# A hybrid decoder layer on one core: the order of work between the output projection and the up projection

## The chip, the cores and the metric

The kernel runs on one core of one Trainium2 chip. The metric is the device time of one execution in microseconds (us). Three runs of the kernel before took 1426.49, 1427.42 and 1429.19 us; the median is 1427.42.

Engines are named as the profile names them: PE is TensorE (PEld its weight loads), DVE is VectorE, ACT is ScalarE, POOL is GpSimd, SP is SyncE, which only issues transfers here. Each engine works through its own instructions in a fixed order and waits on semaphores of the others.

## The reference, cut to what matters

One layer: three groups of heads mix the sequence (not touched here), then

```python
h = h + jnp.concatenate([o_a, o_b, o_c], axis=-1) @ w_out[l]
h = h + conv_glu_ffn(rmsnorm(h, norm_ffn_g[l]), ffn_up[l], ffn_conv_w[l], ffn_conv_b[l], ffn_down[l])
gate = jax.nn.sigmoid(rmsnorm(h, norm_ple_g[l]) @ ple_gate[l])
h = h + gate * (p[l] @ ple_proj[l])

def rmsnorm(x, g):
    xf = x.astype(jnp.float32)
    y = xf * lax.rsqrt(jnp.mean(xf * xf, axis=-1, keepdims=True) + NORM_EPS)
    return (y * g.astype(jnp.float32)).astype(x.dtype)

def conv_glu_ffn(hn, w_up, conv_w, conv_b, w_down):
    u = hn @ w_up
...
    return (jax.nn.silu(gate) * val) @ w_down
```

The sequence has 1024 positions, the model 1024 columns, `D_FF` is 2816. The part left out of `conv_glu_ffn` is a causal depthwise convolution of width 3 over `u` (uc), whose halves are gate and val. All is float32.

## The kernel before, in words

Data lie transposed: a tile holds 128 columns of the model and all 1024 positions, so h is eight tiles h0 to h7, and a half is 512 positions (one bank of PSUM in float32).

**Products in split precision.** Every operand of a product is split into a high part (a copy of reduced width, `hi`, made by ACT as CAST) and a low part (source minus high part, `lo`, made by DVE or POOL as TENSOR_TENSOR). A product is three matmuls: high by high (L137), high weight by low data (L139), low weight by high data (L141) in `mm3`; in the up projection the three stand in `mul` (L1302). The weights' parts are `whi` and `wlo` (L114, L116), six buffers each in rotation.

**Output projection** (`phase_out`). `rows(m, halves)` makes row m of `@ w_out` for the named halves: 24 products a half into a bank pair `dp` (two in rotation), then DVE adds the bank to h (L1232) and ACT writes h out (L1233). Rows 0 and 1 are made for both halves at once, then rows 2 to 7 for the first half, then rows 2 to 7 for the second.

**Norm factors.** ACT squares the h tiles of a half, DVE sums them in `acc` (L216). `rstd` sums acc over partitions with four small matmuls (L183), DVE scales the sum (L186), POOL raises it to -1/2 (L190). `rstd_spread` spreads the factor over all partitions with four transposing matmuls (L196) into a bank `pb`. DVE then multiplies each h tile by the gain and pb (L1328, `ffn_norm`), and for the first half also splits it into the operands p1 (tiles 0 to 3) and p2 (tiles 4 to 7), called t0 to t15 in the profile (even numbers high, odd low). Before, the first half's factors are made in one piece between row 2 and row 3 of the second half, and the second half's in one piece behind row 7.

**Input embedding.** `p @ ple_proj` needs nothing of h, and is placed here: `pe_load` brings the two halves of p and of the weight (`praw`, two buffers) and splits them (`peh`, `pel`); `embed(m)` makes column m with 12 products, ACT copies the bank to `pst` (L1272, two buffers) and writes it out as `pe` m (L1273). Columns 0 to 4 go to the `dp` banks, 5 to 7 to the banks `bv` of the up projection.

**Operands of the up projection.** The up projection is one level of Strassen's scheme: 22 units f of column blocks, seven products each with the operands p1 to p7. `ffn_operands` makes, out of the normed tiles, the operands p6 and p5 (tiles tp6, tp5), and after the embedding's tiles are freed p7, p3 and p4 (tp7, tp3, tp4; `h` and `l` mark high and low part). The first two units' products with p1 and p2 are made here too; between them ACT keeps the p1 result as `e` (`keep_first`, L1390), since p2 adds into the same bank `bg`.

**Units** (`phase_up`). A unit has two bank pairs, G (`bg`) and V (`bv`). Its weights are sums of the four blocks of the weight: `s7`, `s6`, and for the third product `s6 + s2` (L1416), which may be made only when the sixth product's low part has been taken from s6. `x` (L1465) is e plus the second half of G, where the fifth product lies; the third product then adds into that half. L1467 adds x and the first half of V; the fourth product then adds into that half of V.

**What sets the order.** A scheduler puts the instructions of each engine in order by the place in the program and by dependence. `tc.issue_after(i)` holds an instruction behind the instruction i, `tc.high_priority(offset)` moves it forward by that many places.

## Time and profile before

| | |
|---|---|
| median of three runs | 1427.42 us |
| profiled execution | 1426.41 us, span 1424.6 us |
| mean granted clock of TensorE | 0.992 |
| PE busy | 1381.9 us (97%) |
| DVE busy | 1066.8 us (75%) |
| ACT busy | 602.5 us (42%) |
| POOL busy | 392.5 us (28%) |
| second half of the output projection to the first units | about 600 to 720 us of the span |

A row of the timeline has the start in us from the span's start, the duration, engine, line, operation, what it writes and reads, the count of like instructions that follow each other, and in brackets how long the engine stood idle before and what ended that. A wait is put down to the semaphore that came last by the records. A row of the waits has the waiting engine and line, what it waited for, then us in total, times, and the longest. Two matmuls overlap in the records, so their pace is read from start to start. The span begins with the first instruction and leaves out 1.8 us of the execution's time.

### The profile page before, as it was taken

To read this page: it belongs to the slowest core of one execution; us is meant where nothing else is said; L and a number is where in the kernel's file an instruction comes from. 1 tells how busy PE (TensorE), PEld (TensorE's weight loads), DVE (VectorE), ACT (ScalarE), POOL (GpSimd) and SP (SyncE) were. 2 spreads that over 40 slices of the span, in tenths; PEclk is the share of its full clock that TensorE was granted. 3 is DMA by queue.
4 is the path that set the end of the run, shared out by engine and by line. 5 is a ranking of instruction groups with operands and counts; after the bars stand their busy time and mean duration, and the time that the engine had idled before them with its cause. 6 is when DMAs were issued, how large, how long until landed. Compare 5 with 4: busy or idle time off the path is not lost.

```text
span 1424.6 us, 22342 instructions
## 1 busy us (share of the span) xinstructions
PE 1381.9 (97%) x8642; PEld 1118.0 (78%) x8642; DVE 1066.8 (75%) x1629; ACT 602.5 (42%) x1015; POOL 392.5 (28%) x286
## 2 busy tenths in 40 slices
PE   8989999999999999999999999999999999999996
PEld 6768777777778768787788888888888888888885
DVE  7597363964666796468788888898888799778675
ACT  7411323123155485254544444443434444455542
POOL 5321012210122141221244544454543000002431
PEclk9999999999999999999999999999999999999998
DMA  6124111240432211753332233333324963441443
GB/s 220 45 82 119 61 46 61 81 119 32 154 143 104 84 61 40 262 178 117 119 111 91 94 106 102 106 102 111 112 96 147 356 214 111 126 141 47 135 158 113
DMA packets 80122, 167.61 MB, mean 118 GB/s; under 512 B 19984, under 2 KB 22288, under 8 KB 80016
## 3 DMA queue, kind: packets, MB, share of 16 engines
q1 hardware_dynamic: 66496, 146.52, 30.6%
q10 hardware_dynamic: 12656, 16.52, 3.4%
q0 software_dynamic: 864, 3.15, 0.6%
q8 instruction: 68, 1.11, 0.3%
q14 instruction: 38, 0.31, 0.1%
HBM read 119.76 MB, written 46.40 MB: 117 GB/s over the span
## 4 chain that ended last, share of the span: by engine, by line
PE 48%; issue 3%; DVE 2%; POOL 1%; ACT 1%; DMA 0%; POOLq 0%; ACTq 0%; DVEq 0%
PE bg L1302 16%; PE bv L1302 12%; PE bv L1596 7%; PE bg L1596 7%; PE dp L141 1%; PE dp L137 1%; PE dp L139 1%; POOL wlo L116 1%; PE bv L137 0%; PE bv L139 0%; PE bv L141 0%; DVE h L1692 0%; POOL xh L162 0%; DVE gt L1691 0%; ACT whi L114 0%
## 5 line engine op out<-in xcount | busy, mean ns | idle before, releaser
L137 PE MATMUL dp<-xh,whi 128*128 128x512 f32 x544 | 189.2, 408 | 6.9 <-DVE r L501 2.9
L139 PE MATMUL dp<-xl,whi 128*128 128x512 f32 x544 | 182.7, 396 | 0.8 <-DVE xl L411 0.8
L141 PE MATMUL dp<-xh,wlo 128*128 128x512 f32 x544 | 181.1, 394 | 0.0
L116 POOL TENSOR_TENSOR wlo<-wraw,whi 128x512 fp32r<-128x512 f32 x60 | 81.6, 1360 | 321.4 <-ACT whi L114 257.1
L116 POOL TENSOR_TENSOR wlo<-raw,whi 128x512 fp32r<-128x512 f32 x84 | 134.7, 1622 | 76.0 <-ACT whi L114 76.0
L114 ACT CAST whi<-wraw 128x512 fp32r<-128x512 f32 x120 | 72.8, 617 | 155.7 <-PE dp L139 107.3
L1302 PE MATMUL bg<-t,whi 128*128 128x512 f32 x352 | 133.3, 389 | 0.0
L137 PEld LDWEIGHTS dp<-xh,whi 128*128 128x128 f32 x544 | 99.4, 189 | 34.9 <-issue 6.2
L139 PEld LDWEIGHTS dp<-xl,whi 128*128 128x128 f32 x544 | 102.2, 189 | 23.8 <-DVE xl L411 1.1
L141 PEld LDWEIGHTS dp<-xh,wlo 128*128 128x128 f32 x544 | 102.7, 189 | 22.9 <-issue 0.8
L116 POOL TENSOR_TENSOR wlo<-s,whi 128x512 fp32r<-128x512 f32 x44 | 64.0, 1454 | 175.0 <-ACT whi L114 175.0
L1596 PE MATMUL bg<-t,whi 128*128 128x512 f32 x308 | 95.3, 390 | 0.0
L1596 PE MATMUL bv<-t,whi 128*128 128x512 f32 x308 | 94.8, 389 | 0.0
L114 ACT CAST whi<-raw 128x512 fp32r<-128x512 f32 x88 | 52.6, 619 | 94.3 <-issue 48.3
L114 ACT CAST whi<-s 128x512 fp32r<-128x512 f32 x66 | 38.9, 620 | 121.4 <-PE bg L1302 113.6
L1302 PEld LDWEIGHTS bg<-t,whi 128*128 128x128 f32 x352 | 66.1, 188 | 13.6
L190 POOL TENSOR_TENSOR rst<-rst,mhalf 128x4 f32<-128x4 f32 (+1 forms) x9 | 9.9, 1102 | 235.6 <-DVE rst L186 218.5
L1302 PE MATMUL bg<-t,wlo 128*128 128x512 f32 x176 | 67.2, 389 | 0.0
L1596 PEld LDWEIGHTS bv<-t,whi 128*128 128x128 f32 x308 | 57.9, 188 | 11.9
L1596 PEld LDWEIGHTS bg<-t,whi 128*128 128x128 f32 x308 | 57.8, 188 | 12.0
L1592 ACT CAST t<-t 128x512 fp32r<-128x512 f32 x77 | 47.8, 622 | 45.5 <-PE bv L1596 31.8
L116 DVE TENSOR_TENSOR wlo<-wraw,whi 128x512 fp32r<-128x512 f32 x60 | 49.7, 829 | 20.6 <-ACT whi L114 20.4
(417 smaller groups left out, 3415.1 us busy)
## 6 DMA issues: line engine op xcount, KB each, us to landing
raw<-in_ffn_up_dram SPq DMA_DIRECT2D x44, 512.0 KB, 3.5
wraw<-in_w_in_dram SPq DMA_DIRECT2D x28, 512.0 KB, 3.4
z<-zst SPq DMA_DIRECT2D x18, 512.0 KB, 2.8
gb<-ct SPq DMA_DIRECT2D x33, 256.0 KB, 2.2
t<-gb SPq DMA_DIRECT2D x33, 256.0 KB, 2.7
t<-gt SPq DMA_DIRECT2D x33, 256.0 KB, 2.7
zl<-z SPq DMA_DIRECT2D x16, 512.0 KB, 4.2
wraw<-in_ple_gate_dram SPq DMA_DIRECT2D x16, 512.0 KB, 3.4
```

The costliest lines, as they stand in the source:

```text
L114: self.cast = nc.scalar.copy(hi, src).ins
L116: eng.tensor_tensor(lo, src, hi.bitcast(F32), ALU.subtract)
L137: nc.tensor.matmul(ps[hf], wh, xh[hf], start=first, stop=False)
L139: nc.tensor.matmul(ps[hf], wh, xl[hf], start=False, stop=False)
L141: nc.tensor.matmul(ps[hf], wl, xh[hf], start=False, stop=last)
L190: nc.gpsimd.tensor_tensor(r2, r, self.mhalf[:, :n], ALU.pow)
L1302: nc.tensor.matmul(ps, w[part == 2][:, s], X[k][part == 1], start=start and k == part == 0, stop=k == 3 and part == 2, skip_group_check=no ...
L1592: nc.scalar.copy(xh, x)
L1596: nc.tensor.matmul(ps[m], wt[part == 2][:, m * P:(m + 1) * P], (xh, xl)[part == 1], start=k == part == 0, stop=k == NK - 1 and part == 2)
```

## The change

Five edits, none of which adds or drops a product, a copy or a transfer:

1. The first half's factors are made up to POOL's power behind row 2, and spread behind row 3. The loop over rows starts at 4 and takes two `pe_load` in its first turn.
2. The second half's factors are made and spread inside the embedding's second column: the sum behind its first six products, the spread behind its last six.
3. ACT's copy of an embedding column is moved forward in the order by 400 places.
4. In `ffn_operands` the second part of the first units' weights is split ahead of the p1 products; p7 is split first, the copies `e` are held behind the last cast before them, p3 is split in two pairs between, and p4 behind the p2 products.
5. In unit 1 the sum `s6 + s2` is held behind x of unit 0.

```diff
@@ phase_out
         rows(2, (1,))
-        pb = self.rstd_bcast(acc, 1.0 / 1024, EPS, self.mxp)
+        ps, pb = (self.mxp.tile([P, n], F32, tag="mx", name=self.nm("ps_ss")) for n in (4, HT))
+        r = self.rstd(ps, (acc,))
+        rows(3, (1,))
+        pb = self.rstd_spread(r, pb)
...
-        for m in range(3, ND):
+        for m in range(4, ND):
             rows(m, (1,))
             for _ in range(2):
                 next(norm, None)
-            if parts:
-                self.pe_load(pwp, *parts.pop(0))
+            for _ in range(2 if m == 4 else 1):
+                if parts:
+                    self.pe_load(pwp, *parts.pop(0))
         for m in range(ND):
             self.sq_acc(acc, self.h[m][:, HT:], m == 0)
-        pb = self.rstd_bcast(acc, 1.0 / 1024, EPS, self.mxp)
+        ps, pb = (self.mxp.tile([P, n], F32, tag="mx", name=self.nm("ps_ss")) for n in (4, HT))
         self.ffn_first()
+        r = []
+        hooks = {(1, 0): lambda: r.append(self.rstd(ps, (acc,))), (1, 1): lambda: self.rstd_spread(r[0], pb)}
         for m in range(5):
-            self.embed(m, pw, px, self.dps.tile([P, T], F32, tag="dp", name=self.nm("dp")))
+            self.embed(m, pw, px, self.dps.tile([P, T], F32, tag="dp", name=self.nm("dp")), hooks)
@@ embed
+            if (m, k) in hooks:
+                with self.tc.issue_after(self.step):
+                    hooks[m, k]()
         t = self.wpool.tile([P, T], F32, tag="wraw", name=self.nm("pst"), bufs=2)
-        self.nc.scalar.copy(t, ps)
+        with self.tc.high_priority(offset=400):
+            self.nc.scalar.copy(t, ps)
@@ ffn_operands
-        self.mul(*[(d["G"][:, :HT], d["w1"], self.TX["p1"], True) for d in first])
-        for d in first:
-            self.keep_first(d)
         for d in first:
             d["w2"] = self.split2(d["raw"][:, HT:], V)
-        self.mul(*[(d["G"][:, :HT], d["w2"], self.TX["p2"], False) for d in first])
+        self.mul(*[(d["G"][:, :HT], d["w1"], self.TX["p1"], True) for d in first])
...
-        for n, B in (("p7", B12), ("p3", B22), ("p4", B21)):
-            for k in range(4):
-                split(n, k, B[k])
+        for k in range(4):
+            split("p7", k, B12[k])
+        for i, d in enumerate(first):
+            with self.tc.issue_after(self.cast):
+                self.keep_first(d)
+            for k in (0, 1):
+                split("p3", 2 * i + k, B22[2 * i + k])
+        self.mul(*[(d["G"][:, :HT], d["w2"], self.TX["p2"], False) for d in first])
+        for k in range(4):
+            split("p4", k, B21[k])
@@ w, in phase_up
             if n == "3":
-                V.tensor_tensor(d["s"]["3"], d["s"]["3"], d["s"]["2"], ALU.add)
+                with ExitStack() as order:
+                    if d["f"] == 1:
+                        order.enter_context(self.tc.issue_after(self.units[0]["x"]))
+                    V.tensor_tensor(d["s"]["3"], d["s"]["3"], d["s"]["2"], ALU.add)
```

(`self.step` is the last matmul of `mm3`, `self.cast` the last cast of `op_split`, `d["x"]` the instruction that makes x.)

**TensorE at the second half's factors.** Before (dp_1170 and dp_1172 are the embedding's first two columns; the peh numbers ending in 22 and 44 are the two halves of the embedding's weight, 30 and 44 after):

```order
L137 MATMUL dp_1172_6584<-peh_1122_6340,peh_1133_6391 128x512 x2
L183 MATMUL ps_ss_1158_6538<-few_78,acc_5825 128x1 x4
L139 MATMUL dp_1172_6584<-pel_1123_6341,peh_1133_6391 128x512 x2
L196 MATMUL ps_ss_1159_6539<-cst_76,rst2_1161_6546 128x128 x4
L141 MATMUL dp_1172_6584<-peh_1122_6340,pel_1134_6392 128x512 x2
```

Now:

```order
L137 MATMUL dp_1170_6572<-peh_1130_6377,peh_1133_6385 128x512 x2
L139 MATMUL dp_1170_6572<-pel_1131_6378,peh_1133_6385 128x512 x2
L141 MATMUL dp_1170_6572<-peh_1130_6377,pel_1134_6386 128x512 x2
L183 MATMUL ps_ss_1158_6538<-few_78,acc_5825 128x1 x4
L137 MATMUL dp_1170_6572<-peh_1144_6436,peh_1148_6477 128x512 x2
L139 MATMUL dp_1170_6572<-pel_1145_6437,peh_1148_6477 128x512 x2
L141 MATMUL dp_1170_6572<-peh_1144_6436,pel_1149_6478 128x512 x2
L196 MATMUL ps_ss_1159_6539<-cst_76,rst2_1172_6585 128x128 x4
```

The sum stands four products later in the second column, and six products instead of two stand between the sum and the spread.

**ACT at the end of the embedding.** Before (pst_1187, 1189 and 1191 are the copies of columns 5, 6 and 7):

```order
L1320 CAST tp6h3_6664<-nu_1183_6695 128x512
L1320 CAST tp5h6_6670<-h2_5795 128x512
L1320 CAST tp5h7_6672<-h3_5796 128x512
L1272 COPY pst_1187_6724<-bv_1186_6711 128x1024
L1272 COPY pst_1189_6740<-bv_1188_6727 128x1024
L1273 DMA pe5_6289<-pst_1187_6724 128x1024
L1273 DMA pe6_6290<-pst_1189_6740 128x1024
L1320 CAST tp7h0_6836<-h0_5793 128x512
L1272 COPY pst_1191_6756<-bv_1190_6743 128x1024
L1320 CAST tp7h1_6838<-h1_5794 128x512
```

and, after the write of column 7 and the cast of tp7h2:

```order
L1390 COPY e_1192_6783<-bg_1184_6709 128x512
L1390 COPY e_1193_6785<-bg_1185_6710 128x512
L1320 CAST tp7h3_6842<-h3_5796 128x512
L1320 CAST tp3h0_6828<-h4_5797 128x512
```

Now, from the copy of column 5 to the first casts of p3 in two pieces:

```order
L1282 COPY pst_1187_6724<-bv_1186_6711 128x1024
L1330 CAST tp5h5_6668<-h1_5794 128x512
L1330 CAST tp5h6_6670<-h2_5795 128x512
L1330 CAST tp6h3_6664<-nu_1183_6695 128x512
L1282 COPY pst_1189_6740<-bv_1188_6727 128x1024
L1330 CAST tp5h7_6672<-h3_5796 128x512
L1283 DMA pe5_6326<-pst_1187_6724 128x1024
L1283 DMA pe6_6327<-pst_1189_6740 128x1024
L1330 CAST tp7h0_6808<-h0_5793 128x512
L1282 COPY pst_1191_6756<-bv_1190_6743 128x1024
L1330 CAST tp7h1_6810<-h1_5794 128x512
```

```order
L1330 CAST tp7h2_6812<-h2_5795 128x512
L1330 CAST tp7h3_6814<-h3_5796 128x512
L1404 COPY e_1196_6832<-bg_1184_6709 128x512
L1330 CAST tp3h0_6800<-h4_5797 128x512
L1330 CAST tp3h1_6802<-h5_5798 128x512
L1404 COPY e_1197_6838<-bg_1185_6710 128x512
```

The copy of column 5 stands ahead of the casts of tp5h5, tp5h6 and tp6h3; all casts of tp7 stand ahead of the two copies e, which lie among the casts of p3. The copy of column 7 still stands ahead of the cast of tp7h1.

**VectorE between the units.** Before (s7_1213 and s6_1214 belong to unit 1, s7_1234 and s6_1235 to unit 2, x_1208 and bv_1206 to unit 0):

```order
L116 TENSOR_TENSOR wlo_1205_6976<-s7_1198_6961,whi_1204_6974 128x512
L1408 TENSOR_TENSOR s7_1213_7029<-raw_1164_6556,raw_1165_6558 128x512
L1455 TENSOR_TENSOR v_1207_6991<-e_1192_6783,bv_1206_6978 128x512
L1410 TENSOR_TENSOR s6_1214_7031<-s7_1213_7029,raw_1165_6558 128x512
L1411 TENSOR_TENSOR raw_1165_6558<-raw_1165_6558 128x512
L1416 TENSOR_TENSOR s6_1214_7031<-s6_1214_7031,raw_1164_6556 128x512
L1465 TENSOR_TENSOR x_1208_7005<-e_1192_6783,bg_1184_6709 128x512
L116 TENSOR_TENSOR wlo_1220_7044<-s7_1213_7029,whi_1219_7042 128x512
L1408 TENSOR_TENSOR s7_1234_7142<-raw_1226_7125,raw_1227_7127 128x512
L1410 TENSOR_TENSOR s6_1235_7144<-s7_1234_7142,raw_1227_7127 128x512
L1467 TENSOR_TENSOR bv_1206_6978<-x_1208_7005,bv_1206_6978 128x512
```

Now, from the sum of the weight's last block on:

```order
L1425 TENSOR_TENSOR raw_1163_6546<-raw_1163_6546 128x512
L1482 TENSOR_TENSOR x_1208_7005<-e_1196_6832,bg_1184_6709 128x512
L1433 TENSOR_TENSOR s6_1214_7031<-s6_1214_7031,raw_1162_6544 128x512
L116 TENSOR_TENSOR wlo_1220_7044<-s7_1213_7029,whi_1219_7042 128x512
L1422 TENSOR_TENSOR s7_1234_7142<-raw_1226_7125,raw_1227_7127 128x512
L1424 TENSOR_TENSOR s6_1235_7144<-s7_1234_7142,raw_1227_7127 128x512
L1484 TENSOR_TENSOR bv_1206_6978<-x_1208_7005,bv_1206_6978 128x512
```

x and the sum have changed places; L1467 (now L1484) stands behind the same instructions as before.

8 lines of the change are left out of this document (4 added, 4 removed).

## The prediction

> **What bounds the kernel now.** I read the view by stages first, then TensorE's waits between 615 and 760 us, then the timelines there, engine by engine. In the loop over the column blocks TensorE has no free time (columns: stretch, us, then busy us of PE, PEld, DVE, ACT, POOL, granted clock, DMA share, GB/s):
>
> ```profile
> 800.00:900.00 100.00, 100.00 (x443) 82.83 (x442) 88.13 (x90) 42.28 (x59) 48.66 (x31) 1.00 0.33 111
> ```
>
> So time that TensorE loses ahead of this loop moves everything behind it. All its named waits there lie where the change works:
>
> ```profile
> PE bg L1302 <- ACT whi L114: 1.9, 1, 1.9
> PE ps_ss L196 <- POOL rst L190: 1.3, 2, 0.8
> PE bv L137 <- ACT pst L1272: 0.8, 1, 0.8
> PE ps_ss L183 <- DVE acc L216: 0.6, 1, 0.6
> PE bv L1302 <- DVE bv L1467: 0.3, 1, 0.3
> ```
>
> These are 4.9 us, but the timeline shows more. I measure from start to start: products that run without a wait follow each other by 0.227 us (0.453 us for a pair).
>
> ```profile
> 629.18 0.39 PE L139 MATMUL dp<-xl,whi 128*128 128x512 f32 x1
> 630.12 0.65 PE L196 MATMUL ps_ss<-cst,rst 128*128 128x128 f32 x4 [0.55 <-POOL rst L190]
> ...
> 659.45 0.61 PE L137 MATMUL dp<-peh,peh 128*128 128x512 f32 x2
> 660.62 1.02 PE L183 MATMUL ps_ss<-few,acc 128*128 128x1 f32 x8 [0.56 <-DVE acc L216]
> 661.50 0.72 PE L139 MATMUL dp<-pel,peh 128*128 128x512 f32 x2
> 662.98 0.65 PE L196 MATMUL ps_ss<-cst,rst 128*128 128x128 f32 x4 [0.76 <-POOL rst L190]
> 663.38 0.99 PE L141 MATMUL dp<-peh,pel 128*128 128x512 f32 x2
> ...
> 667.34 0.62 PE L139 MATMUL dp<-pel,peh 128*128 128x512 f32 x2
> ...
> 680.49 0.39 PE L1302 MATMUL bg<-t,whi 128*128 128x512 f32 x1
> 681.66 0.73 PE L137 MATMUL bv<-peh,peh 128*128 128x512 f32 x2 [0.78 <-ACT pst L1272]
> ...
> 703.10 0.39 PE L1302 MATMUL bv<-tp7h,wlo 128*128 128x512 f32 x1
> 705.43 0.47 PE L1302 MATMUL bg<-tp3h,whi 128*128 128x512 f32 x1 [1.95 <-ACT whi L114]
> ...
> 708.24 0.39 PE L1302 MATMUL bv<-tp6h,whi 128*128 128x512 f32 x1
> 708.98 0.50 PE L1302 MATMUL bv<-tp4h,whi 128*128 128x512 f32 x1 [0.35 <-DVE bv L1467]
> ```
>
> Lost: 630.12 - 629.18 - 0.23 = 0.71; 660.62 - 659.90 = 0.72; 662.98 - 661.95 = 1.03; five pairs from 663.38 to 667.34 take 3.96 instead of 2.27, so 1.69; 0.94 at 681.66; 2.10 at 705.43; 0.51 at 708.98. That is 7.7 us. The 1.69 are no wait: the granted clock is down there.
>
> ```profile
> 664.00:668.00 4.00, 4.00 (x12) 3.13 (x12) 4.00 (x7) 1.02 (x1) 0.00 (x0) 0.62 0.02 9
> ```
>
> **The change, on TensorE.** No product, copy or transfer is added or taken away; all is moved. The first factors' spread (L196) goes behind row 3's 24 products (5.4 us), the factor is there by 630.12 and TensorE comes at 629.41 + 19 x 0.227 = 633.7: minus 0.71. The second acc sum (L183) goes four products back, which is 0.91 us, while the 0.71 brings TensorE forward: it comes at 659.90 - 0.71 + 0.91 = 660.10. It waits for the end of this VectorE queue:
>
> ```profile
> 656.92 0.69 DVE L1232 TENSOR_TENSOR h<-h,dp 128x512 f32<-128x512 f32 x1 [1.29 <-PE dp L141]
> 658.10 1.77 DVE L1416 TENSOR_TENSOR s<-s,raw 128x512 f32<-128x512 f32 x1 [0.48 <-POOL wlo L116]
> 659.79 0.68 DVE L216 TENSOR_TENSOR acc<-acc,sqt 128x512 f32<-128x512 f32 x1
> ```
>
> All three follow row 7's end (its addition is the first row), now 0.71 earlier, so acc lets L183 start at 659.91: no wait, 0.2 to spare. From L183's start to L196's were 2.36 us (660.62 to 662.98); L183's own 0.88 and six products (1.36) now stand between, 2.24, so 0.12 is left of the 1.03. The half-rate stretch follows from a TensorE that, between 659.9 and 663.4, had one pair of products beside L183 and two waits; with nine products there I expect full rate, minus 1.69. Of the embedding products the eighth waits for a bank that ACT copies out; that copy stood behind three casts and now stands ahead of three, so that it ends near 676.2 where TensorE comes at 676.5 (662.46, 0.40 for L196 and five embedding products of 12 x 0.227): minus 0.94.
>
> At 705.43 the page names the cast of a weight. I read it otherwise: tp3's products add into the half of the G bank that x reads, and x ends at 704.61 + 0.68 = 705.29. TensorE starts 0.14 later. x stood behind L1416 of unit 1, which waited for GpSimd; x now goes first. On TensorE alone the sum of all is 7.7 - 0.12 = 7.6.
>
> **The same change on VectorE, which I think decides.** tp4's first product waits for L1467, and L1467 stands at the end of a VectorE queue that is nearly full from the second factors on:
>
> ```profile
> 663.67 5.35 DVE L1328 SCALAR_TENSOR_TENSOR h<-h,par,ps_ss 128x512 f32<-128x512 f32 x8 [1.83 <-PE ps_ss L196]
> ...
> 674.10 0.69 DVE L1321 TENSOR_TENSOR tp6l<-nu,tp6h 128x512 fp32r<-128x512 f32 x1 [1.46 <-ACT tp6h L1320]
> ...
> 687.80 1.29 DVE L1321 TENSOR_TENSOR tp7l<-h,tp7h 128x512 fp32r<-128x512 f32 x2 [2.17 <-ACT tp7h L1320]
> 691.32 0.69 DVE L1321 TENSOR_TENSOR tp7l<-h,tp7h 128x512 fp32r<-128x512 f32 x1 [2.23 <-ACT tp7h L1320]
> ...
> 696.75 0.68 DVE L116 TENSOR_TENSOR wlo<-s,whi 128x512 fp32r<-128x512 f32 x1
> ...
> 702.95 1.74 DVE L1416 TENSOR_TENSOR s<-s,raw 128x512 f32<-128x512 f32 x1 [1.52 <-POOL wlo L116]
> 704.61 0.68 DVE L1465 TENSOR_TENSOR x<-e,bg 128x512 f32<-128x512 f32 x1
> ...
> 708.23 0.69 DVE L1467 TENSOR_TENSOR bv<-x,bv 128x512 f32<-128x512 f32 x1
> ```
>
> Call W the start of the weight's low part at 696.75. From 663.67 to W are 33.1 us, of which three waits take 5.9 (6.1 from issue to issue, since each also breaks an overlap of 0.09): 27.0 us of work. L196 comes at 660.10 + 2.36 = 662.46, 0.52 earlier; so without any wait W would be 663.15 + 27.0 = 690.1. Behind W the chain stays: L1416 starts 6.20 after W, because it needs the low part that GpSimd makes from a sum that VectorE makes after W,
>
> ```profile
> 701.62 1.29 POOL L116 TENSOR_TENSOR wlo<-s,whi 128x512 fp32r<-128x512 f32 x1 [1.34 <-ACT whi L114]
> ```
>
> and L1467 starts 5.28 after L1416, of which 0.60 was x. x now lies in the 1.52 that VectorE waits for GpSimd, so it costs nothing, and tp4 starts 6.20 + 4.68 + 0.75 = 11.63 after W.
>
> What waits does W keep? The three were ACT's doing:
>
> ```profile
> 680.61 1.91 ACT L1272 COPY pst<-bv 128x1024 f32<-128x1024 f32 x2
> 681.64 1.24 ACTq L1273 DMA_DIRECT2D pe<-pst  x2
> 686.23 1.01 ACT L1272 COPY pst<-bv 128x1024 f32<-128x1024 f32 x1 [1.35 <-DMA pe<-pst]
> 689.70 1.07 ACT L1390 COPY e<-bg 128x512 f32<-128x512 f32 x2 [1.41 <-PE bg L1302]
> 693.26 2.19 ACT L1320 CAST tp4h<-h 128x512 fp32r<-128x512 f32 x4
> DMA to landing us min/median/max: 2.6/3.0/4.8
> ```
>
> A copy takes ACT 0.93 us, a cast 0.52. The 1.46 goes: tp6h's first cast no longer stands behind a copy that waits for TensorE. The 2.17 stays in part: tp7h1 still stands behind the eighth embedding copy, and that behind the landing of the sixth's write, whose buffer it takes. In the new order 21 instructions stand between the factors and the last nu (8 at 5.35 / 8 = 0.66, 13 at 0.60: it starts at 676.3 and ends at 676.9); then ACT has a cast, a copy and a cast, and issues the write at about 679.0. From issue to the copy that waited took 4.6 us in the trace (681.64 to 686.23, two writes together); with the median landing it is 3.0. So the eighth copy starts at 682.0 to 683.6 and tp7's second low part 1.6 later, 683.6 to 685.2, where VectorE, 12 instructions behind 676.3, would be at 683.5: a wait of 0.1 to 1.7. The 2.23 goes, since tp7's casts now stand ahead of the e copies; but each e copy takes a place between tp3's casts, and VectorE, at 0.60 an instruction, runs into them for about 0.3 twice. New waits: 0.7 to 2.3.
>
> Sum: 0.52 + 6.1 + 0.60 - (0.7 to 2.3) = 4.9 to 6.5. The write goes out in a pair again, as in the row with 4.6, so I take a value near the lower end, **5.2**. TensorE's 7.6 is more than this, so tp4 waits for the rest: about 2.4 us of idle there, where tp3 waited before. VectorE and GpSimd also collide (L1416 took 1.77 and 1.74 beside a GpSimd low part, 0.68 is a like instruction alone): such collisions lie behind W before and after, and one more or less is 1.1 us either way. That bounds the sum at 3.8 and 7.6.
>
> At no cost: the embedding operands' low parts, drawn forward on VectorE to where it now waits for row 3, while the factor's eight multiplications go back by 3.6 us. The queue holds the same instructions up to row 7's addition, ahead of which 1.29 us were idle; the earlier end of row 7 takes 0.71 of that. If the cover were gone, L183 would be late by what is lacking.
>
> **Base.** The profiled execution took 1426.41 us (span 1424.60), the median of the runs is 1427.42. 1426.41 - 5.2 = 1421.2 for an execution like that; on the median, **1422.2 us**. A measurement of this kernel tells about 0.2%, 2.9 us, from no change.
>
> **Rivals.** (a) *VectorE meets no wait and no extra collision*: then TensorE's 7.6 or VectorE's 7.2 is the gain, 1420.0. For: casts are 0.52 and VectorE's 0.60. Against: the write's landing. 15%.
>
> (b) *The half rate moves to tp4.* In the trace 1.75 us of waits within 3.5 us (660 to 663.4) were followed by 3.9 us at half rate, while 2.10 at once (703.3 to 705.4) were not. A wait of 2 to 3 us at tp4 lies between; if the clock falls, 1.7 go back: gain 3.5, 1423.9. 18%. [...]
>
> (c) *ACT stays the bound*: the eighth copy's write lands late (4.8 or more) and the e copies come late, so VectorE keeps its 6.1 us of waits. Then only 0.52 + 0.60 come, 1426.3: no change. 12%.
>
> (d) *Slower.* The last half of the embedding weight is now cast ahead of t0's cast on ACT. Its load can be issued only when VectorE has done the first half's low parts (about 631.1), and behind that cast ACT holds the t casts, row 7's weights and the squares that feed acc. The load took 3.3 us:
>
> ```profile
> praw<-in_ple_proj_dram SPq DMA_DIRECT2D x1, 512.0 KB, 3.3
> ```
>
> That gives 634.4, as ACT comes. About 0.8 us (0.58 of idle left, 0.2 to spare) is covered, the rest delays L183 one for one. It decides from 641, ten us after the issue; at 645 the time would be 1431. Against it: three times the measured time would be needed. 5%.
>
> **Chances.** Forecast 50%. Faster by over 0.2% are the forecast, (a) and most of (b): 0.79; within it (c) and the rest: 0.16; slower 0.05. Range: from (a) with the spread of the runs, 1419.2, to between (b) and (c), 1425.7. The forecast's own is 1420 to 1423.7.
>
> **What would show it.** Right: no wait before L196 near 634 and under 0.3 before it near 662; clock 1.00 from 660 to 668; no wait at the eighth embedding product; tp3's first product behind tp7 without a wait, and a wait of 2 to 3 us before tp4 on L1467's line; W near 692. Wrong: a W near 690 with TensorE still late (the work count), tp3 still late with x done (my reading of 705.43), or half rate behind tp4 (b).

## The result and the profile after

Six runs of the changed kernel took 1419.75 to 1422.87 us, median 1421.09; six of the kernel before, beside them, 1425.96 to 1429.41, median 1426.95. The ratio is 0.9953, 95% interval 0.9941 to 0.9964: 5.9 us faster by the medians, 5.1 to 8.4 by the interval. The prediction was 1422.2 (1419.2 to 1425.7), a gain of 5.2. The profiled execution took 1421.0 us, span 1419.2.

TensorE's waits between 615 and 760 us, of which the kernel before had five (columns as there):

```profile
PE bv L1312 <- DVE bv L1484: 1.2, 1, 1.2
```

One is left, before tp4. L1484 is the addition into V (L1467 before), L1482 is x, L1433 the sum s6 + s2, L1338 the factor's multiplications, L1312 the products. TensorE's timeline of the change:

```profile
628.38 0.94 PE L183 MATMUL ps_ss<-few,acc 128*128 128x1 f32 x8
...
634.78 0.60 PE L196 MATMUL ps_ss<-cst,rst 128*128 128x128 f32 x4
...
661.09 0.95 PE L183 MATMUL ps_ss<-few,acc 128*128 128x1 f32 x8
...
663.39 0.64 PE L196 MATMUL ps_ss<-cst,rst 128*128 128x128 f32 x4
...
699.04 0.39 PE L1312 MATMUL bv<-tp7h,wlo 128*128 128x512 f32 x1
699.26 0.39 PE L1312 MATMUL bg<-tp3h,whi 128*128 128x512 f32 x1
...
701.98 0.39 PE L1312 MATMUL bv<-tp6h,whi 128*128 128x512 f32 x1
703.58 0.50 PE L1312 MATMUL bv<-tp4h,whi 128*128 128x512 f32 x1 [1.21 <-DVE bv L1484]
```

Neither factor makes TensorE wait, tp3 follows tp7 at the normal pace of 0.22 us, and tp4 loses 703.58 - 701.98 - 0.23 = 1.37 us. The granted clock (third column from the right, 1.00) does not fall behind the second factors:

```profile
660.00:664.00 4.00, 4.00 (x25) 3.35 (x24) 0.90 (x3) 1.36 (x2) 1.01 (x1) 1.00 0.66 233
664.00:668.00 4.00, 4.00 (x20) 3.27 (x19) 3.93 (x6) 1.61 (x2) 0.00 (x0) 1.00 0.40 162
```

VectorE's timeline, the rows that answer to those of the prediction:

```profile
664.07 5.35 DVE L1338 SCALAR_TENSOR_TENSOR h<-h,par,ps_ss 128x512 f32<-128x512 f32 x8 [1.83 <-PE ps_ss L196]
...
686.77 1.29 DVE L1331 TENSOR_TENSOR tp3l<-h,tp3h 128x512 fp32r<-128x512 f32 x2 [0.49 <-ACT tp3h L1330]
688.30 1.29 DVE L1331 TENSOR_TENSOR tp3l<-h,tp3h 128x512 fp32r<-128x512 f32 x2 [0.23 <-ACT tp3h L1330]
...
691.92 0.68 DVE L116 TENSOR_TENSOR wlo<-s,whi 128x512 fp32r<-128x512 f32 x1
...
696.74 0.69 DVE L1482 TENSOR_TENSOR x<-e,bg 128x512 f32<-128x512 f32 x1
698.13 1.76 DVE L1433 TENSOR_TENSOR s<-s,raw 128x512 f32<-128x512 f32 x1 [0.70 <-POOL wlo L116]
...
702.84 0.68 DVE L1484 TENSOR_TENSOR bv<-x,bv 128x512 f32<-128x512 f32 x1
```

Of the three waits on ScalarE (1.46, 2.17, 2.23) none is left; two small ones are new (0.49, 0.23). x lies ahead of the sum, in what was the wait for GpSimd.

**One measure for all kernels.** The start of the first factors' product (L183 near 628 us) differs between executions, so I measure from there to tp4's first product, and from there to the end of the span. In the two profiled executions:

| | first factors | tp4 | stretch | tp4 to the end | sum |
|---|---|---|---|---|---|
| before | 627.35 | 708.98 | 81.63 | 715.62 | 797.25 |
| change | 628.38 | 703.58 | 75.20 | 715.62 | 790.82 |

(The span is read to 0.1 us, so the last two columns are good to 0.05.) The stretch gained 6.43 us, and nothing is won or lost behind it. The span gained 5.4, because the changed kernel's execution came to the stretch 1.03 us late, in code that the change does not touch: its TensorE ran at half rate (granted clock 0.50) from 360.36 to 363.78 us. Of the fourteen executions in this document, the four without half rate between 16 and 600 us (before, e1, e3, e7) come to the stretch at 627.29 to 627.40, the ten with such stretches at 628.05 to 632.86.

### The profile page after: what moved, and what is told of

Its sections match the earlier page's. It is cut to its first block, busy times and chain, and to the rows that moved or that the text cites. A ratio compares the mean times of both kernels' runs of the same rounds, so it can differ in the third digit from the quotient of the medians.

```text
span 1419.2 us, 22340 instructions
## 1 busy us (share of the span) xinstructions
PE 1380.7 (97%) x8642; PEld 1117.5 (79%) x8642; DVE 1066.0 (75%) x1629; ACT 603.2 (43%) x1015; POOL 393.3 (28%) x286
## 4 chain that ended last, share of the span: by engine, by line
PE 64%; DVE 4%; issue 3%; POOL 2%; ACT 2%; DMA 1%; SPq 0%; POOLq 0%; ACTq 0%; DVEq 0%
PE bg L1312 17%; PE bv L1312 12%; PE bv L1613 7%; PE bg L1613 7%; PE dp L139 3%; PE dp L137 3%; PE dp L141 3%; PE swq L1143 1%; PE hsc L990 1%; PE zp L137 1%; PE zp L141 1%; PE zp L139 1%; PE swo L1183 1%; PE swt L1169 1%; PE bv L139 1%
## 5 line engine op out<-in xcount | busy, mean ns | idle before, releaser
L1312 PE MATMUL bg<-t,whi 128*128 128x512 f32 x352 | 133.4, 389 | 0.0
L1312 PEld LDWEIGHTS bg<-t,whi 128*128 128x128 f32 x352 | 66.1, 188 | 13.8
L1312 PE MATMUL bg<-t,wlo 128*128 128x512 f32 x176 | 67.5, 389 | 0.0
```

What stands on the lines that cost most here:

```text
L1312: nc.tensor.matmul(ps, w[part == 2][:, s], X[k][part == 1], start=start and k == part == 0, stop=k == 3 and part == 2, skip_group_check=no ...
```

## The experiments

All kernels in one table, times in us from the profiled executions; the ratio to the kernel before is given with its interval where runs were timed. The ratios are of three batches (e1 to e4; the change again and e5 to e7; e9), each with its own runs of the kernel before, so only those of one batch compare closely. The kernel before again, e3 again and e4 again are one execution each.

| kernel | first factors | tp4 | stretch | tp4 to the end | sum | ratio |
|---|---|---|---|---|---|---|
| before, again | 632.86 | 714.56 | 81.70 | 715.64 | 797.34 | |
| change, again | 628.05 | 703.24 | 75.19 | 715.66 | 790.85 | 0.9935 (0.9911 to 0.9959) |
| e1 sum ahead of x | 627.32 | 702.62 | 75.30 | 715.48 | 790.78 | 0.9956 (0.9940 to 0.9973) |
| e2 fifth edit alone | 630.32 | 710.16 | 79.84 | 715.44 | 795.28 | 0.9984 (0.9973 to 0.9995) |
| e3 edits 1, 2 alone | 627.40 | 704.95 | 77.55 | 717.15 | 794.70 | 0.9983 (0.9968 to 0.9999) |
| e3 again (e12) | 631.49 | 709.05 | 77.56 | 715.45 | 793.01 | |
| e4 edits 3, 4 alone | 628.64 | 707.74 | 79.10 | 715.66 | 794.76 | 1.0000 (0.9988 to 1.0012) |
| e4 again (e11) | 629.99 | 710.71 | 80.72 | 715.39 | 796.11 | |
| e5 edit 2 undone | 628.60 | 704.65 | 76.05 | 715.65 | 791.70 | 0.9960 (0.9943 to 0.9976) |
| e6 edit 1 undone | 631.08 | 707.02 | 75.94 | 715.68 | 791.62 | 0.9950 (0.9933 to 0.9967) |
| e7 addition into V earlier | 627.29 | 701.11 | 73.82 | 716.89 | 790.71 | 0.9937 (0.9917 to 0.9957) |
| e9 and x of unit 2 earlier | 628.59 | 702.41 | 73.82 | 715.59 | 789.41 | 0.9938 (0.9913 to 0.9962) |

Two executions of one program agree in the stretch within 0.07 us where the granted clock stays up (change, e3), or falls in both (before). So differences of some tenths can be read from it, which the medians can't tell. One thing must be alike for that: behind the second factors the kernel before (both times), e2 and e4's second execution ran at half rate for 3.4 us, the others did not.

### The change once more (e8)

> The change once more, unaltered, to see how far one execution tells: stretch from the first factors' product to tp4 75.2 us within 0.2, wait before tp4 1.2 to 1.4, and 715.6 us from tp4 to the end of the span. The granted clock of 0.98 from 300 to 400 us, which its first profile showed and others did not, is either there again (then it belongs to this program) or not (then it is one execution's).

```profile
703.24 0.50 PE L1312 MATMUL bv<-tp4h,whi 128*128 128x512 f32 x1 [1.21 <-DVE bv L1484]
```

Stretch 75.19, the same wait, and the granted clock was 1.00 from 300 to 400 us this time. The 0.98 there belongs to one execution.

### What decides: VectorE's queue or TensorE's own waits (e1, e2)

e1 keeps four edits and turns the fifth round; only VectorE's order differs from the change's.

```diff
 def w(d, n):
     if n == "3":
-        with ExitStack() as order:
-            if d["f"] == 1:
-                order.enter_context(self.tc.issue_after(self.units[0]["x"]))
+        if "sum" not in d:
             V.tensor_tensor(d["s"]["3"], d["s"]["3"], d["s"]["2"], ALU.add)
...
+            if f == 1:
+                d["sum"] = V.tensor_tensor(d["s"]["3"], d["s"]["3"], d["s"]["2"], ALU.add).ins
+                with self.tc.issue_after(d["sum"]):
+                    prev["tail"]()
```

(`tail` holds the last four lines of `unit`: x, the seventh product, the addition into V.)

> The change, with the fifth edit turned round: on VectorE unit 1's sum (s6 + s2, which waits for GpSimd) stands ahead of x again, as before the change; all other edits stay. One thing moves with it: unit 2's second sum falls behind the addition into V. I measure in the trace from the first factors' product (L183 near 628 us) to tp4's first product: 81.63 us before, 75.20 after the change. Theory (VectorE's queue up to the addition into V decides; a wait at tp3 and one at tp4 stand for each other): the sum starts near 698.1, when GpSimd's low part is done, x ends near 700.5, tp3 waits about 1.3 us, and tp4's wait of 1.37 is gone: 75.2, within 0.3, and the time stays near 1421. Rival (TensorE's waits add up, and x ahead of the sum is worth the 2.10 that tp3 lost): 77.3, and 1423.2.

Stretch 75.30. VectorE's and TensorE's rows (L1450 is the sum here, L1486 x, L1488 the addition into V):

```profile
697.04 1.77 DVE L1450 TENSOR_TENSOR s<-s,raw 128x512 f32<-128x512 f32 x1 [1.51 <-POOL wlo L116]
698.73 0.67 DVE L1486 TENSOR_TENSOR x<-e,bg 128x512 f32<-128x512 f32 x1
...
701.64 0.68 DVE L1488 TENSOR_TENSOR bv<-x,bv 128x512 f32<-128x512 f32 x1
```

```profile
699.55 0.47 PE L1312 MATMUL bg<-tp3h,whi 128*128 128x512 f32 x1 [1.21 <-ACT whi L114]
...
702.62 0.39 PE L1312 MATMUL bv<-tp4h,whi 128*128 128x512 f32 x1
```

tp3 loses 1.37 us, as tp4 did in the change, and tp4 nothing: the wait only changed its place. The rival's 2.1 us did not come. Part of this is owed to unit 2's second sum, which went behind the addition into V: left ahead of it, at 0.60 us from start to start, tp4 would by an estimate from these rows have waited about 0.4 us as well. It also bears on what tp3 waits for. As in the kernel before, the page names ScalarE's cast of a weight. x and that cast both follow the sum and end at 699.40 and 699.52, so this row can't separate them. The changed kernel can. There the same cast starts at

```profile
699.98 0.62 ACT L114 CAST whi<-s 128x512 fp32r<-128x512 f32 x1 [2.12 <-DVE s L1433]
```

and tp3 had started at 699.26. The cast is not what tp3 needs. x, into whose bank tp3's products add, ends 0.15 us ahead of tp3 in e1 and 0.14 in the kernel before, and 1.8 us ahead of it in the change, where tp3 does not wait.

One thing shows in the order of the instructions alone: the fifth edit, merely taken out of the change, leaves all engines in the very same order, since the scheduler puts x ahead of the sum by itself once the third and fourth edits are there. In the change it does nothing.

e2 is the kernel before with the fifth edit alone:

```diff
+        with ExitStack() as order:
+            if d["f"] == 1:
+                order.enter_context(self.tc.issue_after(self.units[0]["x"]))
             V.tensor_tensor(d["s"]["3"], d["s"]["3"], d["s"]["2"], ALU.add)
```

> The kernel before with the fifth edit alone: unit 1's sum goes behind x, nothing else changes. Stretch from the first factors' product to tp4, 81.63 us before. Theory: tp3 follows tp7 with no wait (2.10 less), but tp4 waits about 2 us where it waited 0.51, because the addition into V comes only 0.60 earlier: 81.0, time 1426.3, a change that the median can hardly tell. Rival (TensorE's waits add up): 79.5, time 1424.9.

Stretch 79.84, near the rival's 79.5 and not the theory's 81.0. The rows, TensorE and then VectorE (L1419 is the sum):

```profile
710.16 0.50 PE L1302 MATMUL bv<-tp4h,whi 128*128 128x512 f32 x1 [0.72 <-DVE bv L1470]
```

```profile
705.72 0.75 DVE L116 TENSOR_TENSOR wlo<-s,whi 128x512 fp32r<-128x512 f32 x1 [0.69 <-ACT whi L114]
706.39 1.78 DVE L1419 TENSOR_TENSOR s<-s,raw 128x512 f32<-128x512 f32 x1
```

tp4 still waits for the addition into V, so VectorE decides here too; my size was wrong. Not x alone went ahead of the sum but unit 1's seventh low part as well, and one of the collisions with GpSimd was gone (in the kernel before L1408 took 1.67 us at 705.92, beside a GpSimd low part, and L1410 0.69 at 707.62, beside none): from the sum to the addition into V are 3.02 us (706.39 to 709.41) instead of 5.28, while the sum itself starts 6.64 instead of 6.20 behind W. That makes 1.82, and 1.79 were measured. The rival came near by its number, by another way.

### The two halves of the change (e3, e4)

e3 is the kernel before with the factors' edits (1 and 2) alone, e4 with ScalarE's (3 and 4) alone; their diffs are the hunks of the change, in short:

```diff
@@ e3: phase_out and embed
-        pb = self.rstd_bcast(acc, 1.0 / 1024, EPS, self.mxp)
+        r = self.rstd(ps, (acc,))
+        rows(3, (1,))
+        pb = self.rstd_spread(r, pb)
...
+        hooks = {(1, 0): lambda: r.append(self.rstd(ps, (acc,))), (1, 1): lambda: self.rstd_spread(r[0], pb)}
```

```diff
@@ e4: embed and ffn_operands
-        self.nc.scalar.copy(t, ps)
+        with self.tc.high_priority(offset=400):
+            self.nc.scalar.copy(t, ps)
...
+            split("p7", k, B12[k])
+        for i, d in enumerate(first):
+            with self.tc.issue_after(self.cast):
+                self.keep_first(d)
+            for k in (0, 1):
+                split("p3", 2 * i + k, B22[2 * i + k])
```

> The kernel before with the first two edits alone: both factors' products are spread behind other products, and the embedding operands' loads are drawn forward as in the change; ScalarE's order behind the second factors, and x, stay. In both theories the waits before L196 and L183 and the half rate behind them go, so TensorE is 4.1 us early at 667. Theory A (it is ScalarE's order that makes VectorE's three waits of 1.46, 2.17 and 2.23 us, and VectorE decides): of the three at least 3.6 us stay, TensorE gives the gain back at tp3, and the stretch of 81.63 us falls to 78.6 to 81.1; time 1424 to 1426.4. Theory B (ScalarE was late only because TensorE was late: its copies waited for products): the three waits shrink as TensorE is earlier, and the whole gain comes: 77.5, time 1422.9.

> The kernel before with the third and fourth edits alone: ScalarE's bank copies ahead, seventh operand ahead of the first results' copies; factors and x stay. Theory A: VectorE's three waits go or fall to under 1 us in all, W (the start of the weight's low part, 696.75 before) comes near 691.6, and then TensorE decides: its losses up to 667 (0.71, 0.72, 1.03, 1.69 at half rate) stay, those behind (0.94, 2.10, 0.51) go: the stretch of 81.63 us falls to 78.1, with no wait at tp3 and tp4; time 1423.5. Theory B (ScalarE's order costs little by itself; it is late because TensorE is): W comes 1 to 2 us earlier, the stretch is 79.6 to 80.6, time 1425 to 1426.

e3's stretch is 77.55 and 77.56, as theory B has it: TensorE's 4.1 us came through (and x went ahead of the sum in this order too, which I had not expected). But of the three waits on ScalarE one grew, and TensorE now waits longest at tp4 (in order VectorE, ScalarE, TensorE):

```profile
687.30 1.89 DVE L1330 TENSOR_TENSOR tp7l<-h,tp7h 128x512 fp32r<-128x512 f32 x3 [2.91 <-ACT tp7h L1329]
```

```profile
685.68 1.08 ACT L1399 COPY e<-bg 128x512 f32<-128x512 f32 x2 [2.01 <-PE bg L1311]
```

```profile
704.95 0.79 PE L1311 MATMUL bv<-tp4h,whi 128*128 128x512 f32 x1 [2.53 <-DVE bv L1476]
```

Of 5.9 us of waits 3.1 stay (2.91 and one of 0.21): half of them went because TensorE filled the banks earlier, half stay because the copies e stand ahead of tp7's casts.

e4's stretch is 79.10. Of the 5.9 us 2.5 stay, in a new place (VectorE, then ScalarE):

```profile
689.47 1.29 DVE L1322 TENSOR_TENSOR tp3l<-h,tp3h 128x512 fp32r<-128x512 f32 x2 [2.30 <-ACT tp3h L1321]
```

```profile
688.33 0.59 ACT L1395 COPY e<-bg 128x512 f32<-128x512 f32 x1 [2.51 <-PE bg L1303]
```

The casts stand in the better order, but tp3's casts now stand behind a copy e, which waits for p1 products of a TensorE that is late. Theory A does not hold: W is 3.4 us earlier instead of 5.1, and tp3 is still 1.33 late. And 79.10 is too good for these edits, since this execution kept the full clock behind the second factors and the kernel before did not. e4's second execution (e11, below) had the half rate there too: its stretch is 80.72 and W comes 1.8 us earlier, which is theory B's 1 to 2 us and its 80.6 within 0.1. So at like clock ScalarE's order alone is worth 0.9 us, the factors' edits alone 4.1 (the half rate that they take away is in it), and both together 6.4: 1.4 us come only where both are there. The medians agree with that order of sizes (1.0000 and 0.9983). In the change VectorE's waits are down to 0.72 in all.

### Each factor's edit undone (e5, e6)

e5 takes back edit 2, e6 edit 1, the rest of the change stays.

```diff
@@ e5
-        r = []
-        hooks = {(1, 0): lambda: r.append(self.rstd(ps, (acc,))), (1, 1): lambda: self.rstd_spread(r[0], pb)}
+        pb = self.rstd_bcast(acc, 1.0 / 1024, EPS, self.mxp)
...
@@ e6
-        r = self.rstd(ps, (acc,))
-        rows(3, (1,))
-        pb = self.rstd_spread(r, pb)
+        pb = self.rstd_bcast(acc, 1.0 / 1024, EPS, self.mxp)
...
-        for m in range(4, ND):
+        for m in range(3, ND):
```

> The change with the second edit undone: the second factors' two products stand where they stood before the change (the acc sum four embedding products earlier than now, the spread after four); the other edits stay, and with this the embedding copies and casts on ScalarE come in a slightly other order. The waits of 0.72 and 1.03 us ahead of L183 and L196 come back; the half rate behind them (1.69 us) may or may not, since e4_act had these waits without it. The spread itself comes no later than now (35.01 us behind the first factors' product), so VectorE starts its run of work as early. Stretch from the first factors' product to tp4: 75.20 us in the change. Theory (VectorE's work waits for ScalarE's copies of banks that TensorE fills, so a late TensorE stalls it in a wait for the first results' copy, as the 2.30 us in e4_act): 76.5 to 78.5, with a VectorE wait of over 1 us at tp3's low parts. Rival (VectorE's queue goes its own way, and the 1.37 us that tp4 waits take up the loss): 75.6 without the half rate.

> The change with the first edit undone: the first factors are spread ahead of row 3's products again, and the embedding operands' loads and low parts go back with it; the other edits stay. Theory (row 7's addition, acc, the second factors and all behind them follow TensorE): the wait of 0.71 us before L196 near 630 comes back and is passed on whole, and the stretch to tp4 goes from 75.20 to 75.9; time 0.7 above the change. Rival (it is covered by the wait at tp4): 75.2, no difference.

e5: the waits of 0.72 and 1.03 are back, without half rate, and the stretch is 76.05. VectorE's wait of e4 is back to the hundredth:

```profile
688.67 1.30 DVE L1329 TENSOR_TENSOR tp3l<-h,tp3h 128x512 fp32r<-128x512 f32 x2 [2.30 <-ACT tp3h L1328]
```

So TensorE's lateness reaches VectorE through the copy e, as the theory has it: W comes 1.69 us later than in the change (65.22 against 63.53 behind the first factors' product). The stretch still came out below the theory's 76.5, because in this order, as in e2, the low part went ahead of the sum, and W to tp4 took 10.83 instead of 11.66. 1.69 less 0.83 are the 0.86 that the stretch grew.

e6: TensorE waits 0.56 before L196 again, and the same 1.21 before tp4:

```profile
633.85 0.65 PE L196 MATMUL ps_ss<-cst,rst 128*128 128x128 f32 x4 [0.56 <-POOL rst L190]
...
707.02 0.50 PE L1308 MATMUL bv<-tp4h,whi 128*128 128x512 f32 x1 [1.21 <-DVE bv L1480]
```

Stretch 75.94, 0.74 more than the change: the 0.71 is passed on whole. The wait at tp4 covers nothing of it, since VectorE's work starts with the factors and is late by as much.

### When the clock falls (e10, e11, e12)

The prediction took 1.69 us of half rate behind the second factors as the waits' doing. e4 had the same waits at full rate, so three kernels were run again unaltered: the kernel before, e4 and e3.

> The kernel before, unaltered, for the half rate behind 663 us. In its first profile the half-rate stretches begin and end on a grid of 3.413 us (663.63 - 15.10 = 190 x 3.413), and one follows a grid cell in which TensorE worked little. Theory (where the grid falls is chance, and the two waits of 0.72 and 1.03 us may lie in one cell or be cut in two): the same waits at 33.3 and 35.6 us behind the first factors' product, and half rate behind them only if one cell holds most of both; it may be absent. Rival (the program's own waits set it): half rate from about 36.3 us behind the first factors' product, for 3.4 us, as before.

> The kernel of e4_act, unaltered, for the same question: it had the two waits of 0.72 and 1.03 us and kept full rate. Theory (chance of the grid): half rate may follow this time; then the stretch from the first factors' product to tp4 is longer than its 79.10 us by up to 1.7. Rival (the program sets it): full rate again, 79.1.

> The kernel of e3_factors, unaltered: it lost 2.69 us before tp4 and then ran at half rate for 3.4 us. Theory (a grid cell with TensorE busy for about a third is followed by half rate; a wait of 2.5 us that is cut in two by the grid leaves both cells at a half or more): half rate behind tp4 or not, by where the cell lies; the wait itself again 2.5. Rival (a wait of this length always brings it): half rate from tp4 on again.

e4 at full rate, and then, with the same waits, at 0.72 (third column from the right):

```profile
664.00:668.00 4.00, 3.73 (x19) 3.16 (x20) 3.04 (x5) 1.02 (x1) 0.22 (x1) 1.00 0.36 143
```

```profile
664.00:668.00 4.00, 3.23 (x13) 2.51 (x13) 1.49 (x4) 0.00 (x0) 1.01 (x1) 0.72 0.66 244
```

Its stretch is 80.72 instead of 79.10. The kernel before was at half rate again (0.60 from 668 to 672, its second factors at 668.48). e3 was the other way round: half rate behind tp4's wait of 2.53 us, and in its second execution none:

```profile
709.05 0.50 PE L1311 MATMUL bv<-tp4h,whi 128*128 128x512 f32 x1 [2.54 <-DVE bv L1476]
709.39 0.40 PE L1311 MATMUL bv<-tp6l,whi 128*128 128x512 f32 x1
```

The view by stages, in windows of 3.41 us, first of the kernel before, then of e3, then of e3 again:

```profile
660.22:663.63 3.41, 2.26 (x15) 1.85 (x16) 0.41 (x2) 0.44 (x1) 1.01 (x1) 1.00 0.79 257
663.63:667.05 3.42, 3.42 (x9) 2.65 (x9) 3.38 (x6) 0.08 (x1) 0.00 (x0) 0.50 0.12 50
```

```profile
701.37:704.78 3.41, 1.05 (x5) 0.54 (x3) 3.34 (x4) 1.24 (x2) 2.70 (x2) 1.00 0.47 154
704.78:708.20 3.42, 3.25 (x8) 2.58 (x9) 2.15 (x4) 1.21 (x1) 0.64 (x1) 0.50 0.00 0
```

```profile
704.95:708.36 3.41, 1.56 (x7) 0.95 (x6) 3.34 (x5) 1.24 (x2) 2.17 (x2) 1.00 0.51 154
708.36:711.77 3.41, 2.72 (x12) 2.26 (x13) 2.32 (x4) 1.05 (x1) 1.17 (x1) 1.00 0.00 0
```

These windows are not chosen freely. Each is counted in steps of 3.413 us from the end of the execution's first half-rate stretch: 15.10 in the kernel before, and 663.63 - 15.10 = 190 x 3.4133; 15.29 in e3, and 704.78 - 15.29 = 202 x 3.4133. The step is read from these traces: one stretch lasts 3.42 us (663.63 to 667.05), and the two distances are whole multiples of 3.4133. The changed kernel's stretch near 360 us fits too (360.36 - 15.62 = 101 x 3.413). I call these steps the grid, and one step a cell. Between 16 and 1400 us the stretches whose place was read begin on this grid and last one cell or two (6.83 us in e3's second execution, from 360.20 to 367.03), and the cell ahead of them, where it was read, had 1.05 to 2.26 us of work. The six executions with the two waits of 0.72 and 1.03 us fit this. In the four that had half rate behind them, one cell held most of both (660.22 to 663.63 above, 665.39 to 668.80 in the kernel before again, 662.62 to 666.03 in e2, 662.31 to 665.72 in e4 again). In the two that had none, e4's first and e5, a cell ended between them by this count, at 661.97 and at 661.61. e4's two cells, and then the one of e4 again:

```profile
658.56:661.97 3.41, 2.85 (x14) 2.06 (x12) 2.71 (x3) 1.69 (x3) 2.05 (x2) 1.00 0.21 79
661.97:665.39 3.42, 2.65 (x17) 2.14 (x18) 0.59 (x2) 0.00 (x0) 1.01 (x1) 1.00 0.89 297
```

```profile
662.31:665.72 3.41, 2.09 (x13) 1.31 (x12) 0.94 (x3) 0.97 (x1) 1.01 (x1) 1.00 0.62 185
```

In e3 the wait lay in one cell, in which TensorE was busy 1.05 of 3.41 us; in its second execution the grid cut the wait in two, and 1.56 were left busy. A cell need not be without work for half rate to follow: e3's had 1.05 us of products. Where the limit lies was not shown. Cells with 1.38 us busy (changed kernel, 357 to 360) and less were followed by half rate; of two cells near 1.56, both in e3's second execution, one was (1.58, 356.79 to 360.20) and one was not; the kernel before's with 2.26 was, in which most of the 15 instructions counted are the small ones of L183 and L196, while the changed kernel's cell with tp4's wait (701.70 to 705.11), with 2.20 of ordinary products, was followed by a granted clock of 1.00. So the busy time in the profile does not by itself tell them apart; that small products count for less would fit, and is not shown.

### A better version (e7, e9)

The wait left at tp4 is for an addition behind three instructions that nobody needs so early. e7 moves it ahead of them:

```diff
-            V.tensor_tensor(d["V"][:, HT:], x, d["V"][:, :HT], ALU.add)
+            d["t7"] = V.tensor_tensor(d["V"][:, HT:], x, d["V"][:, :HT], ALU.add).ins
...
+            if d["f"] == 1 and n == "7":
+                with self.tc.issue_after(self.units[0]["t7"]):
+                    return self.split2(d["s"][n], V)
             return self.split2(d["s"][n], V if n in "7" else G)
```

> The change with one more move: on VectorE unit 0's addition into V, on which tp4 waits, goes ahead of unit 1's seventh low part and unit 2's first two sums (a cast on ScalarE moves with it, ahead of a table load). If the 1.37 us that TensorE loses before tp4 are all that is left in the passage: no wait at tp4, the stretch from the first factors' product falls from 75.20 to 73.83, and the time to 1419.7 (1.4 below the change). If the three held instructions are needed in time: TensorE waits for a weight of unit 1 or 2 instead, behind tp4, by up to 2 us, and the time stays near 1421.

tp4 comes without a wait, stretch 73.82 as expected, but tp4 to the end takes 716.89. TensorE loses most of the gain again 31 us later, 0.87 us at one place (TensorE, then VectorE):

```profile
732.07 0.50 PE L1312 MATMUL bg<-tp3h,whi 128*128 128x512 f32 x1 [0.71 <-DVE x L1485]
```

```profile
730.13 1.28 DVE L1498 SCALAR_TENSOR_TENSOR ct<-bv,ncw,ct 128x1022 f32<-128x1022 f32 x1
731.33 0.68 DVE L1485 TENSOR_TENSOR x<-e,bg 128x512 f32<-128x512 f32 x1
```

It is not one of the held weights that is late but x of the next unit but one, behind a convolution that nobody waits for. By the medians nothing was won (1420.85, against 1421.29 of the change in the same batch). e9 is e7 with the convolution behind it:

```diff
-                conv(prev, 1)
-                gate(prev)
+                if f != 2:
+                    conv(prev, 1)
+                    gate(prev)
...
             d["x"] = V.tensor_tensor(x, d["e"], d["G"][:, HT:], ALU.add).ins
+            if f == 2:
+                with self.tc.issue_after(d["x"]):
+                    conv(prev, 1)
+                    gate(prev)
```

> The kernel of e7_t7_first with one more move: on VectorE, x of unit 2 goes ahead of unit 1's second convolution (its two scalar-tensor-tensor instructions and what follows them), whose last part it stood behind in e7, where tp3 of unit 1 then lost 0.87 us at 732. Theory (VectorE's queue sets TensorE's next wait wherever an instruction that TensorE needs stands behind others): the wait of 0.87 goes, no new one comes up to 740, and from the first factors' product to the end of the span there are 1.2 us less than the change has (75.19 + 715.66 = 790.85): 789.6; time about 1420, against 1421.1. Rival (VectorE's work itself is short of room for the first units): the wait comes back at a later addition, and the end stays within 0.3 of 790.85.

(The tp3 at 732 us, called unit 1's there, is unit 2's.)

```profile
729.94 0.69 DVE L1486 TENSOR_TENSOR x<-e,bg 128x512 f32<-128x512 f32 x1 [2.63 <-PE bg L1312]
730.55 1.28 DVE L1502 SCALAR_TENSOR_TENSOR ct<-bv,ncw,ct 128x1023 f32<-128x1023 f32 x1
```

x now waits for TensorE, TensorE waits for nothing up to 760, and the sum is 789.41, 1.4 less than the change's. Six runs: median 1419.75 (1418.5 to 1425.0), against 1421.09 of the change. The profile shows the gain; by the medians the two can hardly be told apart, and the ratios' intervals overlap.

## Why the prediction was right, point by point

**VectorE decides, and W.** Right. The sum in the prediction can be laid beside three pieces of the stretch. The factor's multiplications start 36.32 us behind the first factors' product before (663.67 - 627.35) and 35.69 in the change: 0.63, foreseen 0.52. From there to W are 33.08 and 27.85: 5.23, foreseen 6.1 less 0.7 to 2.3, of which I took 2.0. From W to tp4 are 12.23 and 11.66 (11.63 foreseen): 0.57, foreseen 0.60. Together 6.43 against 5.2. That W stands at 691.9 where I wrote "near 692" is half luck: this execution came 1.03 us late to the stretch, and W is 5.86 earlier by its own count.

**The term that was mis-sized** is the new waits: 0.87 us (6.1 - 5.23) where I took 2.0. The waits behind the e copies were as foreseen (0.49 and 0.23, "about 0.3 twice"). The wait at tp7's second low part, 0.1 to 1.7, did not come at all. ScalarE's rows in the change:

```profile
678.05 0.33 ACTq L1283 DMA_DIRECT2D pe<-pst  x1
678.47 1.01 ACT L1282 COPY pst<-bv 128x1024 f32<-128x1024 f32 x1
...
682.15 0.62 ACT L1330 CAST tp7h<-h 128x512 fp32r<-128x512 f32 x1 [2.16 <-DVE h L1385]
682.68 1.00 ACT L1282 COPY pst<-bv 128x1024 f32<-128x1024 f32 x1
```

I let the sixth column's write go out at 679.0, behind the copy and the cast that stand ahead of it in the order; in this execution, 1.03 us late, that would be 680.0, as the cast ahead of it (679.37) ends. It went out at 678.05, 2 us sooner, before that copy (678.47) had begun. The landing was near the upper end I gave: in e3 a copy that waited for it came 4.53 us behind the issue (677.61 to 682.14), which here is 682.6, and the eighth copy, at 682.68, stands right behind the cast ahead of it, which waited for VectorE's tile. Had the write gone at 680.0, the copy would by the same 4.53 have come near 684.5, and VectorE, which took tp7's second low part at 684.4, would have waited about 1.7 us for the cast behind it. That is an estimate from these rows, and more than the whole error of the term.

**Wait at tp4.** Its place and its releaser were right, its length was not: 1.37, foreseen 2.4. It follows from the same term, 7.81 - 6.43. TensorE's own losses are confirmed by e7 and e9, which have none: 81.63 - 73.82 = 7.81, foreseen 7.6.

**Half rate.** Gone as forecast, but the reason was incomplete. The two waits alone do not tell it: of six executions with these waits four had it (before twice, e2, e4's second), two had not (e4's first, e5), and only in these two had a cell of the grid ended between the waits. It lasted 3.42 us, not the 3.9 that I read. So up to 1.6 us of the 6.43, by e4's pair, depend on whether the kernel before has it; both its executions had the half rate, and how long its stretch is without was not seen.

**Rivals.** (a) did not come: VectorE met the two waits. e7 and e9 reach its gain in the stretch by other moves, with those waits still there. (b), half rate behind tp4, did not come: the wait cost 1.37 us where I had 2.4, and the cell with it, 2.20 us busy, was followed by full rate (1.00 from 705.11 to 708.52). e3, which lost 2.69 us there, had half rate behind it in its first execution and none in its second. My argument that 2.10 us at once are spared was wrong: e3's wait of 2.53 us at once was followed by half rate. In the kernel before, a cell ended at 704.59, inside the wait at tp3 (703.48 to 705.43), and the cells on both sides of it had 2.32 and 2.57 us of products; that this spared it is my estimate from e3's two executions, and was not shown. (c): ScalarE did not stay the bound. (d): the late load did come late, and ScalarE waited 1.39 us for it:

```profile
632.08 0.33 SPq L1290 DMA_DIRECT2D praw<-in_ple_proj_dram  x1
636.82 1.14 ACT L1293 CAST peh<-praw 128x512 fp32r<-128x512 f32 x2 [1.39 <-DMA praw<-in_ple_proj_dram]
```

The issue is where I put it (631.1, and 1.03 for this execution), but the load took 4.7 us instead of 3.3. So ScalarE's cast came 1.4 us later than the 634.4 I expected, by this execution's count, and well ahead of 641, where by my sum it would have cost something. The embedding's split at no cost, with it, was right.

**The 0.60 for x** was right in the change and would not have carried over: alone, on the kernel before, the same edit gave 1.8 (e2), and within the change it gives nothing, because the order is the same without it.

## What to carry to other kernels

When two engines are both nearly full in a passage, don't add one engine's waits: follow the queue whose last instruction the other waits for, and expect the rest of the gain to turn up as a wait there. Where engine A fills banks that B copies and C waits for B, an order for B and an earlier A can be worth more together than apart: here 0.9 us for the order and 4.1 for the earlier A, but 6.4 for both (by the medians none, about 2, and about 6). After such a change look at the next wait for an instruction that stands behind work nobody needs yet; each of the two moves in e7 and e9 was one such.

## What the runs showed of the hardware that I had not expected

- Half rate started on a grid of 3.413 us, 101, 190 and 202 steps behind the end of a first stretch near 15 us in three executions, and between 16 and 1400 us it lasted 3.42 or 6.83 us where it was read. Whether a given wait was followed by it differed between executions of one program, and went with where a cell ended. A single profile with or without it says little: two waits of 0.72 and 1.03 us had it four times in six, a wait of 2.5 us once in two.
- A transfer that ScalarE issues went out ahead of ScalarE's own work: the write at 678.05 went out before a copy (678.47) that stands two places ahead of it in the order.
- Two executions of one program agreed in an 80 us stretch within 0.07 us, while they came to its start up to 5.5 us apart (627.35 and 632.86). The later one's granted clock was 0.97 from 300 to 400 us and 0.99 from 400 to 600, the earlier one's 1.00 in both.
